# The seven-product pairs of an FFN: token sums traced ahead of the third chunk into buffers of their own, bank evacuations ranked above weight casts

## The chip, the cores and the metric

The kernel runs on one core of a Trainium2 chip. The metric is the device time of one execution in microseconds (us). Before the change the median of three runs is 990.08 us (989.32 to 993.01).

## The reference

Two layers of a streaming encoder on 256 tokens of width 1024, in float32. Each layer has three sub-layers: a feed-forward block (FFN), a mixer of attention and mLSTM, and a second FFN. What matters here is the FFN, of which four are computed:

```python
def _swiglu(h, w_in, w_out):
    gate, up = jnp.split(h @ w_in, 2, axis=-1)      # 1024 -> 2 x 2816
    return (jax.nn.silu(gate) * up) @ w_out         # 2816 -> 1024

x += 1/2 * post(SwiGLU_1(pre(x)))
x += post(W_out [DiffAttn | mLSTM](pre(x)))
x += 1/2 * post(SwiGLU_2(pre(x)))
```

`pre` and `post` are RMS norms. The weights are read from HBM once in each sub-layer.

## The kernel before

**Products.** Every product of float32 numbers is made of three TensorE matmuls on rounded halves, high and low: xh·wh, xh·wl, xl·wh (L471 to L473). So each weight has to be split on the chip. A piece of weights is 1 MB and is fetched on SyncE's queue (`fetch`, three buffers `wr`); each of its two halves is cast by ScalarE into `wh` (L296) and then subtracted by VectorE into `wl` (L297) (`halved`). This split runs through the whole kernel: 372 such pairs of instructions.

**The FFN.** The 2816 hidden columns are eleven chunks of 256. Chunks 0 and 1 come first, then a list of steps runs:

```python
STEPS = "I2 O0 I3 O1 P4 O2 I6 O3 I7 O4 O5 P8 O6 O7 I10"
```

`I` is the input product of a chunk (banks `ptr` for I2, `pin` for I3, in turn), `O` adds a chunk's part to the output banks `bk`, and `P` is a pair of chunks made with seven products instead of eight, in the manner of Strassen. After an `I` step `ffn_hidden` makes h: ScalarE's silu into `sil`, then VectorE multiplies by the other half of the bank (L598), and with that the bank is free. `ffn_planes` turns h around for the output product: ScalarE copies planes (L605), SyncE starts a transposing DMA (L607), ScalarE copies the result into `hT` (L609), and it is split into `hh` and `hl` (L624, L625). The last chunk, I10, is made the other way round (`in_turned`, `ffn_turned`), and behind it stands the ending, in which PE's order is written by hand.

**A pair.** P4 and P8 need sums of weights (`pair_blocks`, L314, VectorE; then 14 halves are split) and sums of tokens (`pair_tokens`): s1 to s4, ten VectorE instructions (L344 to L352) and for each sum a cast on ScalarE (L624, out `both`) and a subtraction on VectorE (L625, out `both`). The token sums are made once in an FFN, at P4, and P8 uses them again. Each of the seven products is twelve matmuls (L705). P1 and P2 use the tokens as they are and share one `pin` bank, so P1's result has to be copied out (`p1`, L717) before P2 adds to the bank; P5 (s1) and P6 (s2) go into a `ptr` and the other `pin` bank, P7 (s3) into the second `ptr` bank, to which P4 later adds, and P3 (s4) adds to P5's. `u`, `v`, `sil` and `h` take the results out.

**What sets the order.** The program is traced in the order of the code, and a scheduler then places each engine's instructions by its own timeline and a priority, which follows the order of tracing; `high_priority()` ranks a block ahead of all else. Each engine then runs its list strictly in order. Tiles come from rings: `u`, `v` and `sum` share a ring of five, "ev", with `h`, `planes`, `turned`, `hT` and others; what has no ring of its own, `sil` and `p1` among them, is in "k2" with four.

Of the kernel before, what the change touches and what calls it, by code (L numbers as in the profile page):

```python
# [20 lines left out]
AF = mybir.ActivationFunctionType  # L21
ALU = mybir.AluOpType
# [3 lines left out]
P = 128  # L26
# [11 lines left out]
END = (8, 9, 10)  # L38
# [97 lines left out]
class _Trunk:  # L136
# [12 lines left out]
        return f"{s}_{self.n}"  # L149


    TAGS = {"kwn": ("kwn", 1), "aT0": ("aT0", 1), "aT1": ("aT1", 1)}
    for _n in ("nat", "ra", "rb", "rv", "tmp", "y", "so", "xg", "h", "planes", "turned", "hT", "u", "v", "sum"):
        TAGS[_n] = ("ev", 5)

    def t2(self, nm, shape=(P, 512), dt=F32):
        tag, bufs = self.TAGS.get(nm, ("k2", 4))
        return self.k2.tile(list(shape), dt, tag=tag, bufs=bufs, name=self.name(nm))
# [502 lines left out]
    def ffn(self, pre, gi_post):  # L661
        xT, r = pre

        def in_piece(t, kh, pin, w):
            xh, xl = xT[t][kh]
            for k in range(4):
                self.mm3(pin, xh[:, k, :], xl[:, k, :], *self.cols(w, k),
                         start=kh == 0 and k == 0, stop=kh == 1 and k == 3)
# [23 lines left out]
        def ready(h):  # L692
            hT = self.ffn_planes(h.rearrange("p t j -> p (t j)"))
            return self.ffn_split([hT[:, t] for t in range(NT)])
# [7 lines left out]
        def product(b, x, w, new):  # L702
            for k in range(4):
                for n, (st, mv) in enumerate(((x[0], 0), (x[0], 1), (x[1], 0))):
                    self.nc.tensor.matmul(b, st[:, k, :], self.cols(w, k)[mv], start=new and k == n == 0,  # L705
                                          stop=k == 3 and n == 2, skip_group_check=True)

        def pair(c):


            tt, stt = self.nc.vector.tensor_tensor, self.nc.vector.scalar_tensor_tensor
            w = self.pair_blocks()
            b1, b2, b3, b4 = self.bank_pin(), self.bank_pin(), self.bank_tr(), self.bank_tr()
            s1, s2, s3, s4 = sums
            product(b1, xT[0][0], w["P1"], True)
            p1 = self.t2("p1")
            self.nc.scalar.activation(p1, b1, AF.Copy)  # L717
            product(b4, s1, w["P5"], True)
            product(b2, s2, w["P6"], True)
            u, v, h0, sil = self.t2("u"), self.t2("v"), self.t2("h"), self.t2("sil")  # L720
            tt(u, b2, p1, op=ALU.subtract)
            product(b3, s3, w["P7"], True)
            tt(v, u, b3, op=ALU.subtract)
            tt(v, v, b4, op=ALU.add)
            product(b1, xT[0][1], w["P2"], False)
            self.func(sil, b1, AF.Silu, scale=r[0])
            product(b4, s4, w["P3"], False)
            tt(h0, b4, u, op=ALU.add)
            stt(h0, h0, r[0], sil, op0=ALU.mult, op1=ALU.mult)
            hT = [self.ffn_planes(h0)]  # L730
            product(b3, xT[1][1], w["P4"], False)
            tt(u, b3, u, op=ALU.subtract)
            self.func(u, u, AF.Silu, scale=r[1])
            stt(v, v, r[1], u, op0=ALU.mult, op1=ALU.mult)
            hT.append(self.ffn_planes(v))
            for j in range(2):
                hs[c + j] = self.ffn_split([h[:, j] for h in hT])

        hs, po = {}, []
# [20 lines left out]
        else:  # L760
# [6 lines left out]
            h = self.t2("h", (P, NT, 256))  # L767
# [12 lines left out]
            h = self.t2("h", (P, NT, 256))  # L780
# [2 lines left out]
            in_piece(1, 1, pb1, w1[1])  # L783
            self.ffn_hidden(pb1, r[1], h[:, 1])
            hs[1] = ready(h)
        both, sums, swap = list(self.both), None, 0
        for step in STEPS[:-1]:
            c = int(step[1:])
            if step[0] == "P":
                sums = sums or self.pair_tokens(both)  # L790
                pair(c)
            elif step[0] == "I":
                if c == 3:
                    g = self.load_gpost(gi_post)
                    yield "middle"
                ws = [self.piece(), self.piece()]
                pins = [self.bank_pin() if swap else self.bank_tr() for _ in range(NT)]
                swap = 1 - swap
                for kh in range(2):
                    for t in range(NT):  # L800
                        in_piece(t, kh, pins[t], ws[kh])
                chunk(c, pins)
            else:
                if not po:
                    po = [[self.bank_bk() for _ in range(2)] for _ in range(NT)]
                wo = self.piece()
                for t in range(NT):
                    out_part(c, t, hs[c], wo)
        ws = [self.piece(), self.piece()]
        rows = self.token_scales(r)  # L810
        last = [self.piece() for _ in END[:-1]]
        banks = [[self.bank_pin() for _ in range(2)], [self.bank_tr() for _ in range(2)]]
        in_turned(banks, ws, both)

        yield "ending"
        hs[END[-1]] = self.ffn_turned(banks, rows)
        last.append(self.piece())
        for c, wo in zip(END, last):
            out_part(c, 0, hs[c], wo)
# [63 lines left out]
class _Mixer:  # L883
# [325 lines left out]
    def scores(self, t, h0):  # L1209

        tr, nc = self.tr, self.tr.nc
        nk, nh = P * (t + 1), 4 // (t + 1)
        if h0 == 0:
            self.aT[t] = tr.t2(f"aT{t}", (P, t + 1, 4, P))
            self.mx = tr.small("mx", (P, 2, 4))
            self.lsum[t] = tr.small("lsum", (P, 2, 4))
        hs = slice(h0, h0 + nh)
        pcs = [tr.bank_bk((P, nh, nk)) for _ in range(2)]
        for h in range(nh):
            for c in range(2):  # L1220
                rows = slice(c * 64, c * 64 + 64)
                self.mm(pcs[c][:, h, :], self.qkT[0][rows, h0 + h, t * P:(t + 1) * P],
                        self.qkT[1][rows, h0 + h, 0:nk], start=True, stop=True)
        for c in range(2):
            nc.vector.memset(pcs[c][0:64, :, nk - 64:nk], BIG)
            nc.vector.tensor_reduce(self.mx[:, c, hs], pcs[c], axis=AX.X, op=ALU.max, negate=True)
        if t:
            p = [tr.t2("p", (P, 2, nk)) for _ in range(nh)]
        else:
            ts = [tr.t2("p", (P, 2, 2, nk)) for _ in range(nh // 2)]  # L1230
            p = [ts[h // 2][:, h % 2] for h in range(nh)]
        self.p[t, h0] = p
        for h in range(nh):
            for c in range(2):
                tr.func(p[h][:, c, :], pcs[c][:, h, :], AF.Exp, bias=self.mx[:, c, h0 + h:h0 + h + 1],
                                accum_out=self.lsum[t][:, c, h0 + h:h0 + h + 1])

    def combine(self, t, h0):

        tr, nc, l = self.tr, self.tr.nc, self.l  # L1240
        nk, nh = P * (t + 1), 4 // (t + 1)
        hs = slice(h0, h0 + nh)
        lsum, aT = self.lsum[t], self.aT[t]
        c1 = tr.small("c1", (P, nh))
        nc.vector.reciprocal(c1, lsum[:, 1, hs])
        self.stt(c1, c1, tr.neglam[:, l:l + 1], lsum[:, 0, hs], op0=ALU.mult, op1=ALU.mult)
        ptr = tr.bank_tr((P, t + 1, nh, P))
        for h in range(nh):
            p = self.p[t, h0][h]
            self.stt(p[:, 0, :], p[:, 1, :], c1[:, h:h + 1], p[:, 0, :], op0=ALU.mult, op1=ALU.add)  # L1250
            for kt in range(t + 1):
                self.T(ptr[:, kt, h, :], p[:, 0, kt * P:(kt + 1) * P], tr.ident)
        self.act(aT[:, :, hs, :], ptr, AF.Copy)

    def attend(self, t):
        tr, l = self.tr, self.l
        po = tr.bank_bk((P, 4, P))
        for h in range(4):
            for kt in range(t + 1):
                self.mm(po[:, h, :], self.aT[t][:, kt, h, :], self.vd[:, kt, h * P:(h + 1) * P],  # L1260
                        start=kt == 0, stop=kt == t)
        ss = tr.small("ssa", (P, 4))
        for h in range(4):
            self.act(tr.junk_tile(P), po[:, h, :], AF.Square, scale=2.0 ** -3.5, accum_out=ss[:, h:h + 1])
        l2 = tr.small("l2", (P, 4))
        self.tt(l2, self.lsum[t][:, 0, :], self.lsum[t][:, 0, :], op=ALU.mult)
        self.stt(ss, l2, EPS, ss, op0=ALU.mult, op1=ALU.add)
        sc = tr.rsqrt(ss, 4)
        y = tr.t2("y", (P, 4, P))
        self.tt(y, po, sc.unsqueeze(2).broadcast_to([P, 4, P]), op=ALU.mult)  # L1270
        self.y[t] = y
# [113 lines left out]
```

## Time and profile before

| | |
|---|---|
| median of three runs | 990.08 us (989.32 to 993.01) |
| the profiled execution | 990.41 us, its span 988.6 us |
| TensorE (PE) busy | 950.4 us, 96% of the span |
| VectorE (DVE) busy | 788.2 us, 80% |
| ScalarE (ACT) busy | 669.5 us, 68% |
| mean granted PE clock | 0.983 of full |
| HBM read | 177.01 MB, 180 GB/s over the span |

Busy shares are means over the whole kernel. PE is the engine on which the end rests nearly everywhere, so what counts is the time in which PE waits or runs at a lower clock, and where that lies.

### The profile page before, as it was taken

The numbers are of one execution on the slowest core, as the hardware profiler recorded it, in microseconds if no ns is written. First come the engines' busy times: TensorE is split into PE (matmuls) and PEld (weight loads), VectorE is DVE, ScalarE is ACT, GpSimd is POOL, SyncE is SP. The second block draws the span as 40 slices with busy tenths as digits, with TensorE's granted clock in tenths as the row PEclk, the third lists the DMA queues.
The fourth block names the chain that finished last, engine by engine and source line by source line (L and its number), as shares of the span: only waits on it lengthen the run. The fifth ranks groups of instructions, "written<-read, shape, count | busy, mean of one in ns | idle before, by whom it ended". The sixth has DMA issues, their size and how long they took to land.

```text
span 988.6 us, 12155 instructions
## 1 busy us (share of the span) xinstructions
PE 950.4 (96%) x4427; PEld 778.7 (79%) x4427; DVE 788.2 (80%) x1097; ACT 669.5 (68%) x1033; POOL 29.3 (3%) x55
## 2 busy tenths in 40 slices
PE   9989999899999998999999799999999999899997
PEld 7867888787888876888788678888888888678886
DVE  6798797589766799698577977977898687997964
ACT  8875686478765775686567747765778468656862
POOL 2000000000010000000000000000000200000000
PEclk9998999999999999999999999999999999999999
DMA  8945668435352745757638446583364438556551
GB/s 324 340 130 198 211 213 291 116 127 193 129 213 85 280 141 194 237 171 272 196 118 308 149 167 202 185 304 101 128 234 140 159 135 298 178 208 196 170 178 43
DMA packets 69882, 189.34 MB, mean 192 GB/s; under 512 B 45274, under 2 KB 46426, under 8 KB 49086
## 3 DMA queue, kind: packets, MB, share of 16 engines
q1 hardware_dynamic: 69246, 187.95, 56.0%
q8 instruction: 35, 0.57, 0.2%
q10 hardware_dynamic: 576, 0.61, 0.2%
q14 instruction: 25, 0.20, 0.1%
HBM read 177.01 MB, written 1.05 MB: 180 GB/s over the span
## 4 chain that ended last, share of the span: by engine, by line
PE 73%; DVE 10%; ACT 8%; DMA 6%; issue 3%; SPq 0%; POOLq 0%; DVEq 0%; ACTq 0%
PE ptr L705 9%; PE bk L473 8%; PE bk L472 8%; PE bk L471 8%; PE pin L471 8%; PE pin L473 8%; PE pin L472 8%; PE pin L705 5%; DVE wl L297 5%; DMA turned<-planes 4%; ACT wh L296 3%; DMA wr<-in_w_dram 2%; PE ptr L471 2%; PE ptr L472 2%; PE ptr L473 2%
## 5 line engine op out<-in xcount | busy, mean ns | idle before, releaser
L297 DVE TENSOR_TENSOR wl<-wr,wh 128x1024 fp32r<-128x1024 f32 x324 | 386.6, 1219 | 69.4 <-ACT wh L296 68.6
L296 ACT ACTIVATE wh<-wr 128x1024 fp32r<-128x1024 f32 x324 | 331.2, 1053 | 96.0 <-DMA wr<-in_w_dram 33.6
L471 PE MATMUL pin<-wh,both 128*128 128x512 f32 x432 | 171.3, 398 | 0.0
L473 PE MATMUL pin<-wh,both 128*128 128x512 f32 x432 | 168.4, 390 | 0.0
L472 PE MATMUL pin<-wl,both 128*128 128x512 f32 x432 | 168.4, 390 | 0.0
L473 PE MATMUL bk<-wh,hl 128*128 128x512 f32 x352 | 138.6, 394 | 2.1 <-DVE hl L625 2.1
L471 PE MATMUL bk<-wh,hh 128*128 128x512 f32 x352 | 133.3, 395 | 5.4 <-ACT hh L624 3.1
L472 PE MATMUL bk<-wl,hh 128*128 128x512 f32 x352 | 138.1, 393 | 0.0
L705 PE MATMUL ptr<-wh,both 128*128 128x512 f32 x256 | 88.9, 411 | 11.4 <-ACT both L624 7.5
L473 PEld LDWEIGHTS pin<-wh,both 128*128 128x128 f32 x432 | 81.1, 188 | 17.4
L471 PEld LDWEIGHTS pin<-wh,both 128*128 128x128 f32 x432 | 81.3, 188 | 17.0 <-issue 0.7
L472 PEld LDWEIGHTS pin<-wl,both 128*128 128x128 f32 x432 | 81.2, 188 | 15.5
L609 ACT ACTIVATE hT<-turned 128x1024 uint16<-128x1024 uint16 x40 | 54.9, 1373 | 56.7 <-DMA turned<-planes 56.5
L471 PEld LDWEIGHTS bk<-wh,hh 128*128 128x128 f32 x352 | 66.7, 190 | 21.2 <-ACT hh L624 4.2
L473 PEld LDWEIGHTS bk<-wh,hl 128*128 128x128 f32 x352 | 66.9, 190 | 17.4 <-DVE hl L625 3.4
L472 PEld LDWEIGHTS bk<-wl,hh 128*128 128x128 f32 x352 | 66.8, 190 | 13.8
L705 PE MATMUL pin<-wh,both 128*128 128x512 f32 x192 | 66.7, 409 | 10.2 <-ACT p L717 9.1
L705 PEld LDWEIGHTS ptr<-wh,both 128*128 128x128 f32 x256 | 50.2, 197 | 25.5 <-ACT both L624 9.2
L297 DVE TENSOR_TENSOR wl<-wide,wh 128x1024 fp32r<-128x1024 f32 x48 | 57.7, 1217 | 2.5 <-ACT wh L296 2.1
L296 ACT ACTIVATE wh<-wide 128x1024 fp32r<-128x1024 f32 x48 | 49.4, 1049 | 13.3 <-DVE wide L314 8.0
L625 DVE TENSOR_TENSOR hl<-hT,hh 128x256 fp32r<-128x256 f32 x80 | 30.9, 418 | 32.8 <-ACT hh L624 32.8
L705 PEld LDWEIGHTS pin<-wh,both 128*128 128x128 f32 x192 | 38.1, 199 | 21.0 <-ACT p L717 10.8
(242 smaller groups left out, 1395.6 us busy)
## 6 DMA issues: line engine op xcount, KB each, us to landing
wr<-in_w_dram SPq DMA_DIRECT2D x162, 1024.0 KB, 5.0
gpost<-in_gpost_dram SPq DMA_DIRECT2D x6, 512.0 KB, 6.4
wr<-in_w_dram SPq DMA_DIRECT2D x2, 512.0 KB, 5.6
wr<-in_w_dram SPq DMA_DIRECT2D x3, 256.0 KB, 4.3
x<-in_x_dram SPq DMA_DIRECT2D x3, 256.0 KB, 4.7
turned<-planes SPq DMA_TRANSPOSE x40, 4.4
out_dram<-x SPq DMA_DIRECT2D x2, 256.0 KB, 2.1
x<-in_x_dram SPq DMA_DIRECT2D x2, 128.0 KB, 2.8
```

The source lines that it names most:

```text
L296: ia = nc.scalar.activation(hi, raw, AF.Copy)
L297: iv = nc.vector.tensor_tensor(lo, raw, hi.bitcast(F32), op=ALU.subtract)
L471: mm(ps, xh, wh, start=start, stop=False)
L472: mm(ps, xh, wl, start=False, stop=False)
L473: mm(ps, xl, wh, start=False, stop=stop)
L609: nc.scalar.activation(hT.rearrange("p a b n -> p (a b n)").bitcast(U16).rearrange("p (n u) -> p u n", u=2), turned.rearrange("p (u b) n - ...
L625: self.nc.vector.tensor_tensor(hl, h, hh.bitcast(F32), op=ALU.subtract)
L705: self.nc.tensor.matmul(b, st[:, k, :], self.cols(w, k)[mv], start=new and k == n == 0, stop=k == 3 and n == 2, skip_group_check=True)
```

## The change

It has four parts. The rings: "ev" goes from five to eight buffers and loses `u`, `v` and `sum`, which go into the ring "k2" of four beside `sil` and `p1`; the mixer's `aT` tiles lose their own buffers, go into "ev", and are split into one tile per 128 keys (so that ScalarE has four copies more in the whole kernel). The token sums: `pair_tokens` is called ahead of the loop over STEPS, so ahead of I2, and no longer inside it at P4. The evacuations of a pair (`p1`, `u`, `v`, `sil`, `h0` and the last ones) are put under `high_priority()`, with their tiles allocated ahead of the products. `ffn_turned`, too, is put under `high_priority()`.

```diff
-    TAGS = {"kwn": ("kwn", 1), "aT0": ("aT0", 1), "aT1": ("aT1", 1)}
-    for _n in ("nat", "ra", "rb", "rv", "tmp", "y", "so", "xg", "h", "planes", "turned", "hT", "u", "v", "sum"):
-        TAGS[_n] = ("ev", 5)
+    TAGS = {"kwn": ("kwn", 1)}
+    for _n in ("nat", "ra", "rb", "rv", "tmp", "y", "so", "xg", "h", "planes", "turned", "hT", "aT"):
+        TAGS[_n] = ("ev", 8)
@@ pair
+            ahead = self.tc.high_priority
+            p1, sil, u, v, h0 = self.t2("p1"), self.t2("sil"), self.t2("u"), self.t2("v"), self.t2("h")
             product(b1, xT[0][0], w["P1"], True)
-            p1 = self.t2("p1")
-            self.nc.scalar.activation(p1, b1, AF.Copy)
+            with ahead():
+                self.nc.scalar.activation(p1, b1, AF.Copy)
             product(b4, s1, w["P5"], True)
             product(b2, s2, w["P6"], True)
-            u, v, h0, sil = self.t2("u"), self.t2("v"), self.t2("h"), self.t2("sil")
-            tt(u, b2, p1, op=ALU.subtract)
+            with ahead():
+                tt(u, b2, p1, op=ALU.subtract)
...
@@ ffn
-        both, sums, swap = list(self.both), None, 0
+        both, swap = list(self.both), 0
+        sums = self.pair_tokens(both)
         for step in STEPS[:-1]:
             c = int(step[1:])
             if step[0] == "P":
-                sums = sums or self.pair_tokens(both)
                 pair(c)
...
-        hs[END[-1]] = self.ffn_turned(banks, rows)
+        with self.tc.high_priority():
+            hs[END[-1]] = self.ffn_turned(banks, rows)
@@ combine
-        self.act(aT[:, :, hs, :], ptr, AF.Copy)
+        for kt in range(t + 1):
+            self.act(aT[kt][:, hs, :], ptr[:, kt], AF.Copy)
```

What the scheduler makes of it is seen in the lists of the engines. In the rows below, the number behind a name tells apart the tiles of one name.

VectorE in the first FFN, behind the weights of I2 (`wl_498` before, `wl_524` after). `h_376` is chunk 1's h, `hl_299` and `hl_301` are chunk 0's. Before:

```order
L297 TENSOR_TENSOR wl_498<-wr_492,wh_499 128x1024
L205 TENSOR_TENSOR c_wgc<-c_528,c_wgc 128x16x8
L225 TENSOR_REDUCE c_hot<-c_95 100x4
L598 SCALAR_TENSOR_TENSOR h_376<-pin_326,rs_31_274,sil_377 128x256
L598 SCALAR_TENSOR_TENSOR h_376<-pin_327,rs_36_283,sil_380 128x256
L239 CAST c_hotp<-c_hot 36x256
L625 TENSOR_TENSOR hl_299<-hT_296,hh_298 128x256
```

And after:

```order
L297 TENSOR_TENSOR wl_524<-wr_518,wh_525 128x1024
L344 TENSOR_TENSOR sum_399<-both_129,both_187 128x512
L345 TENSOR_TENSOR sum_400<-both_129,both_187 128x512
L205 TENSOR_TENSOR c_wgc<-c_554,c_wgc 128x16x8
L225 TENSOR_REDUCE c_hot<-c_95 100x4
L598 SCALAR_TENSOR_TENSOR h_376<-pin_326,rs_31_274,sil_377 128x256
L598 SCALAR_TENSOR_TENSOR h_376<-pin_327,rs_36_283,sil_380 128x256
L346 TENSOR_TENSOR sum_399<-sum_399,sum_400 128x512
L239 CAST c_hotp<-c_hot 36x256
L625 TENSOR_TENSOR hl_299<-hT_296,hh_298 128x256
```

The fourteen VectorE instructions of the sums now stand between here and the first weights of P4, among the weights of I2 and I3; before, they stood among the weights of P4.

VectorE in the second FFN (the one behind the first mixer), at P4. `h_3336` before and `h_3365` after are the h of chunk 3, which frees the two `pin` banks of I3; `wl` of `wide`, `wr_3419` and `wr_3462` (before; 3422, 3443, 3465 after) are weights of P4. Before:

```order
L297 TENSOR_TENSOR wl_3444<-wide_3429,wh_3445 128x1024
L598 SCALAR_TENSOR_TENSOR h_3336<-pin_3286,rs_589_2923,sil_3337 128x256
L297 TENSOR_TENSOR wl_3448<-wide_3429,wh_3449 128x1024
L314 TENSOR_TENSOR wide_3429<-wide_3429,wr_3462 128x1024
L297 TENSOR_TENSOR wl_3454<-wr_3419,wh_3455 128x1024
L598 SCALAR_TENSOR_TENSOR h_3336<-pin_3287,rs_614_3010,sil_3340 128x256
L314 TENSOR_TENSOR wide_3429<-wide_3429,wr_3462 128x1024
```

And after:

```order
L297 TENSOR_TENSOR wl_3471<-wr_3465,wh_3472 128x1024
L297 TENSOR_TENSOR wl_3467<-wr_3465,wh_3468 128x1024
L297 TENSOR_TENSOR wl_3475<-wr_3443,wh_3476 128x1024
L314 TENSOR_TENSOR wide_3432<-wide_3432,wr_3465 128x1024
L297 TENSOR_TENSOR wl_3479<-wr_3443,wh_3480 128x1024
L297 TENSOR_TENSOR wl_3485<-wide_3432,wh_3486 128x1024
L598 SCALAR_TENSOR_TENSOR h_3365<-pin_3315,rs_590_2926,sil_3366 128x256
L598 SCALAR_TENSOR_TENSOR h_3365<-pin_3316,rs_615_3013,sil_3369 128x256
```

The first half of the same h moved behind ten more splits and sums of P4's weights, its second half behind seven. It is so in the third and the fourth FFN too; in the first it isn't.

TensorE at the start of the same P4: the last rows of the output step and the first product. `pin_3490` is the bank of P1, `ptr_3496` that of P5, `both_3138` holds s1 and s2, `both_2863` (before) the tokens. Before:

```order
L473 MATMUL bk_3229<-wh_3364,hl_3130 128x512
L705 MATMUL pin_3490<-wh_3422,both_2863 128x512
L705 MATMUL pin_3490<-wl_3421,both_2863 128x512
L705 MATMUL pin_3490<-wh_3422,both_2863 128x512 x2
L705 MATMUL pin_3490<-wl_3421,both_2863 128x512
```

And after:

```order
L473 MATMUL bk_3258<-wh_3393,hl_3133 128x512
L705 MATMUL ptr_3496<-wh_3436,both_3138 128x512
L705 MATMUL ptr_3496<-wl_3435,both_3138 128x512
L705 MATMUL ptr_3496<-wh_3436,both_3138 128x512 x2
L705 MATMUL ptr_3496<-wl_3435,both_3138 128x512
```

In the second, third and fourth FFN the pair now begins with P5 and P7 in the `ptr` banks (24 matmuls), and P1 and P6 in the `pin` banks follow; then comes the output step O2, and then P2. Before, P1 and P2 came first, 24 matmuls in one bank. In the first FFN the order after is P1, P5, P6 and P7 mixed, P2; before, P1, P2, P5, P6, P7.

More of the change, by code (lines that the diff above doesn't have):

```diff
@@ L714, in pair @@
             s1, s2, s3, s4 = sums
+            ahead = self.tc.high_priority
+            p1, sil, u, v, h0 = self.t2("p1"), self.t2("sil"), self.t2("u"), self.t2("v"), self.t2("h")
             product(b1, xT[0][0], w["P1"], True)
-            p1 = self.t2("p1")
-            self.nc.scalar.activation(p1, b1, AF.Copy)
+            with ahead():
+                self.nc.scalar.activation(p1, b1, AF.Copy)
             product(b4, s1, w["P5"], True)
             product(b2, s2, w["P6"], True)
-            u, v, h0, sil = self.t2("u"), self.t2("v"), self.t2("h"), self.t2("sil")
-            tt(u, b2, p1, op=ALU.subtract)
+            with ahead():
+                tt(u, b2, p1, op=ALU.subtract)
             product(b3, s3, w["P7"], True)
-            tt(v, u, b3, op=ALU.subtract)
-            tt(v, v, b4, op=ALU.add)
+            with ahead():
+                tt(v, u, b3, op=ALU.subtract)
+                tt(v, v, b4, op=ALU.add)
             product(b1, xT[0][1], w["P2"], False)
-            self.func(sil, b1, AF.Silu, scale=r[0])
+            with ahead():
+                self.func(sil, b1, AF.Silu, scale=r[0])
             product(b4, s4, w["P3"], False)
-            tt(h0, b4, u, op=ALU.add)
-            stt(h0, h0, r[0], sil, op0=ALU.mult, op1=ALU.mult)
+            with ahead():
+                tt(h0, b4, u, op=ALU.add)
+                stt(h0, h0, r[0], sil, op0=ALU.mult, op1=ALU.mult)
             hT = [self.ffn_planes(h0)]
             product(b3, xT[1][1], w["P4"], False)
-            tt(u, b3, u, op=ALU.subtract)
-            self.func(u, u, AF.Silu, scale=r[1])
-            stt(v, v, r[1], u, op0=ALU.mult, op1=ALU.mult)
+            with ahead():
+                tt(u, b3, u, op=ALU.subtract)
+                self.func(u, u, AF.Silu, scale=r[1])
+                stt(v, v, r[1], u, op0=ALU.mult, op1=ALU.mult)
             hT.append(self.ffn_planes(v))
@@ L1213, in scores @@
         if h0 == 0:
-            self.aT[t] = tr.t2(f"aT{t}", (P, t + 1, 4, P))
+            self.aT[t] = [tr.t2("aT", (P, 4, P)) for _ in range(t + 1)]
             self.mx = tr.small("mx", (P, 2, 4))
@@ L1259, in attend @@
             for kt in range(t + 1):
-                self.mm(po[:, h, :], self.aT[t][:, kt, h, :], self.vd[:, kt, h * P:(h + 1) * P],
+                self.mm(po[:, h, :], self.aT[t][kt][:, h, :], self.vd[:, kt, h * P:(h + 1) * P],
                         start=kt == 0, stop=kt == t)
```

## Prediction

> **What bounds the kernel now.** I read the shares of the engines first, then what PE waits for, then the stretches of the four P4 pairs, then VectorE's list ahead of them.
>
> ```profile
> span 988.6 us, 12155 instructions
> PE 950.4 (96%) x4427; PEld 778.7 (79%) x4427; DVE 788.2 (80%) x1097; ACT 669.5 (68%) x1033; POOL 29.3 (3%) x55
> ```
>
> PE is the bound, with 38 us of the span not busy. The list of what its matmuls waited for shows where:
>
> ```profile
> PE pin L705 <- ACT p L717: 9.1, 4, 3.1
> PE ptr L705 <- ACT both L624: 7.5, 4, 2.5
> PE ptr L705 <- DVE both L625: 3.9, 3, 1.6
> PE bk L471 <- ACT hh L624: 3.1, 2, 1.6
> PE bk L473 <- DVE hl L625: 2.1, 3, 0.9
> ```
>
> The first three rows (20.5 us) are the pair's: P2 waits for the copy of P1 four times, once in each FFN, and P5 to P7 wait for the casts and remainders of the token sums. The last two are mostly the endings. Around the largest of these waits PE's records in the first FFN (start, length, form, idle time before) read:
>
> ```profile
> 67.92 0.63 PE L705 MATMUL pin<-wh,both 128*128 128x512 f32 x1 [3.06 <-ACT p L717]
> 68.35 0.63 PE L705 MATMUL pin<-wl,both 128*128 128x512 f32 x1
> 74.77 0.66 PE L705 MATMUL ptr<-wh,both 128*128 128x512 f32 x1 [2.24 <-ACT both L624]
> 77.43 1.22 PE L705 MATMUL ptr<-wh,both 128*128 128x512 f32 x2 [1.58 <-DVE both L625]
> ```
>
> Behind such a wait the matmuls follow each other at 0.43 us (67.92 to 68.35). The chain of work that ended last gives the same for a group (start, length, what; the first group is right behind the third wait, the second is undisturbed):
>
> ```profile
> 77.43 4.57 PE ptr L705 x10
> ...
> 86.10 2.27 PE ptr L705 x10
> ```
>
> That is 0.457 us a matmul against 0.227, half the clock, until the stretch ends. Ten cost 2.3 us more here, the twelve from 67.92 on about 1.7. So a wait costs itself and about 1.7 us behind it. By stretches (us, PE busy, granted clock; four P4 pairs, then two endings):
>
> ```profile
> 60.00:90.00 30.00, 23.12 (x82) 0.83 0.43 149
> 365.00:395.00 30.00, 25.14 (x100) 0.94 0.53 175
> 555.00:585.00 30.00, 23.72 (x88) 0.89 0.44 150
> 850.00:880.00 30.00, 24.86 (x100) 0.94 0.49 154
> 178.00:193.00 15.00, 12.51 (x47) 0.89 0.34 131
> 478.00:493.00 15.00, 12.76 (x51) 0.89 0.44 149
> ```
>
> In the first, 6.9 us are idle, and the clock falls short of full by 0.17 x 30 = 5.1 us, of which the two groups above are 4.0 (the rest lies over idle time): 10.9 lost. With the same share (0.78) of the other shortfalls of 1.8, 3.3 and 1.8 us the pairs of the other FFNs lose 4.9 + 1.4 = 6.3, 6.3 + 2.6 = 8.9 and 5.1 + 1.4 = 6.5; together 32.6 us. The two endings lose 2.5 + 1.3 and 2.2 + 1.3. This is all that the change can touch; the P8 pairs show no wait.
>
> **Why the pair waits.** VectorE is full there (start to end, its busy time; first the stretch ahead of P4 in the first FFN, then P4, then the stretches ahead of P4 in the other three):
>
> ```profile
> 20.00:62.00 42.00, 35.38 (x44) 1.00 0.85 275
> 62.00:85.00 23.00, 22.96 (x29) 0.78 0.42 148
> 337.40:367.00 29.60, 26.52 (x32) 1.00 0.50 169
> 526.00:555.60 29.60, 27.04 (x32) 1.00 0.54 174
> 824.50:854.30 29.80, 27.15 (x32) 1.00 0.56 175
> ```
>
> The durations of what it does, start to start, are in the chain:
>
> ```profile
> 63.48 1.14 DVE wide L314
> 64.62 3.41 DVE wl L297 x3
> 68.02 0.60 DVE sum L344
> ```
>
> The fourteen instructions of the token sums are 14 x 0.60 = 8.4 us of VectorE, in the middle of P4's weights.
>
> **The change, part by part.** Moving the sums takes 8.4 us out of P4 and puts them into the stretch ahead. That removes the waits for `both`, if VectorE has room there. It has 6.6 us idle in the first FFN (42.00 - 35.38) and only 3.1, 2.6 and 2.7 in the others; the part for which there is no room makes P4's weights late instead. The four casts of the sums on ScalarE (68% busy) move with them, hidden beside the weight casts. No DMA is moved except that in the first FFN two pieces stand ahead of loads of constants that wait for nothing; I cost that at nothing.
>
> First FFN. Of the idle time I count 5.4 us as usable, the waits for hh, lamv and two casts that lie behind the place of the new rows:
>
> ```profile
> DVE hl L625 <- ACT hh L624: 3.0, 1, 3.0
> DVE lamp L216 <- DMA lamv<-in_lam_dram: 1.4, 1, 1.4
> DVE wl L297 <- ACT wh L296: 0.5, 1, 0.5
> DVE c_wgc L205 <- ACT c_wgc L204: 0.5, 1, 0.5
> ```
>
> So VectorE comes to P4's weights 8.4 - 5.4 = 3.0 us late, at 63.0 for the weight that it split at 60.0, and then runs without the sums. PE's new order puts P5 between P1 and P2, so the 3.06 us for P1's copy go. What is late next is v, which reads P7's bank before the product P4 may add to it: from 63.0, in the row of after, eight splits, two sums of weights, two hl, u and three further splits, 13 x 1.14 + 0.7 + 0.6, so v runs from 79.1 to 79.8; PE, from 62.0 with 60 matmuls of the five products and four of O2, is there at 62.0 + 64 x 0.227 = 76.5. A wait of 3.5 with 1.7 behind it: 5.2 in place of 10.9, **-5.7** (ends: -10.9 if v isn't late, 0 if two such waits are left).
>
> Second FFN. The starts in question (PE: first of P4 in the second, third and fourth FFN; VectorE: an h of chunk 1 in each, from which I walk, and the idle times that can still be filled):
>
> ```profile
> L705 PE MATMUL pin<-wh,both x24: 387/394/796, 367.0 to 384.9; 128*128 128x512 f32 x24
> L705 PE MATMUL pin<-wh,both x24: 388/389/628, 555.6 to 575.1; 128*128 128x512 f32 x24
> L705 PE MATMUL pin<-wh,both x24: 388/389/547, 854.3 to 872.6; 128*128 128x512 f32 x24
> 337.00 0.48 DVE L598 SCALAR_TENSOR_TENSOR h<-pin,rs,sil 128x256 f32<-128x256 f32 x1
> 530.62 0.48 DVE L598 SCALAR_TENSOR_TENSOR h<-pin,rs,sil 128x256 f32<-128x256 f32 x1
> 828.69 0.48 DVE L598 SCALAR_TENSOR_TENSOR h<-pin,rs,sil 128x256 f32<-128x256 f32 x1
> ```
>
> Here chunk 3's h is the last thing of I3 and now stands behind ten more of P4's rows, while PE does P5 and P7 (24 matmuls, 5.45 us) and then needs the bank that this h frees. VectorE's list of after from the row of 337.0 to the end of h: 25 splits and sums of weights x 1.135, 14 x 0.605, 4 x 0.34, 6 x 0.4 = 40.6, so 377.6 if no idle time is left, 379.3 with what I cannot place; PE is ready at 367.0 + 5.45 = 372.4. A wait of 5.2 to 6.9, I take 6.0, and 1.7 behind it: 7.7 against 6.3, **+1.4**. Third FFN, by the same walk from 530.62: 33.8, with 0.2 of lag brought along, 564.6; PE ready at 561.0; wait 4.0 with the semaphores' way, and 1.7: 5.7 against 8.9, **-3.2**. Fourth, from 828.69: 32.6, so 861.3 to 861.6; PE ready at 859.8; 2.2 and 1.7: 3.9 against 6.5, **-2.6**. Ends for the three together: +8, if the copy of P1 behind the late bank also holds P2, and -14.
>
> The priority of the evacuations acts where the scheduler had put them behind weight casts; P2 now has O2 or two products ahead of it (at least 24 matmuls, 5.4 us), so the copy's 0.57 us is covered. The cover would be gone only if the copy waits for ScalarE's `hT` of chunk 3, which the late h delays by its transposition; 24 matmuls of P6 and O2 lie over that.
>
> Endings. `ffn_turned` ahead of casts moves the hh for which the output product waits one cast earlier (1.05 us in its row):
>
> ```profile
> L296 ACT ACTIVATE wh<-wr 128x1024 fp32r<-128x1024 f32 x324 | 331.2, 1053 | 96.0 <-DMA wr<-in_w_dram 33.6 <-PE ptr L705 20.1 <-PE bk L473 14.6
> ```
>
> That is about 1.0 in each of the two endings that wait, **-2.0** (0 to -6). The rings and the split `aT`: four ScalarE copies more, in mixers where PE hardly waits: 0 (ends -1 and +2).
>
> The sum: -5.7 + 1.4 - 3.2 - 2.6 - 2.0 = -12.1. Against the profiled execution's 990.41 this is 978.3, and, the median of the runs being 0.3 lower, **978**.
>
> [...]
>
> **The rivals.** (B) The waits nearly all go: VectorE's lag is absorbed, because the weights of P4 are split before PE needs them. Then 32.6 + 4 are gained: 954, or two thirds of it, 966. Against it: VectorE had 3 us idle where 8.4 go. (C) The gain is given back: what the sums cost at P4 is now the lag of weights and of h, in three of four FFNs. With the first FFN at -3, the others at 0 and the endings at nothing: 985 to 995. For it: the three rows of 26.5 to 27.2 busy out of 29.6. (D) Slower: chunk 3's h holds the `pin` banks in three FFNs so long that P1, P6 and then P2 each wait. It decides from the point where each FFN loses 12 us and not 6: one wait of 7, its 1.7, and a second of 3 to 4 for the copy behind `hT`; 3 x 5 = +15, less 8 of the first FFN and the endings, 997. Against it: the walk puts h 1.8 to 5.2 us behind PE, not 7.
>
> **How the numbers follow.** A forecast sum within 966 to 985: 0.64. B below 966: 0.08. C, 985 to 995: 0.17. D above 995: 0.11. A measurement of this kernel tells about 0.5%, 5 us, from no change; so faster (below 985) 0.72, same 0.17, slower 0.11. The range leaves out the larger part of B and the far half of D with the edge of C: 964 to 993.
>
> **What would show it.** Right: at P4 no row of PE waiting for `both` from L624 or L625; in the first FFN one wait of 3 to 4 us at a `ptr` bank for v; in the second one of some 6 us at `pin` for chunk 3's h (L598), in the third 4, in the fourth 2; the endings' waits near 1.5 instead of 2.5. Wrong: if P5 itself waits for its weights, if the copy of P1 still shows with 2 us or more, or if waits appear at P8, in the steps I6 and I7, or in the mixers, where I cost the rings at nothing.

## The result and the profile after

The changed kernel takes 983.55 us in the median (983.13 to 984.71, four runs) against 990.31 us before on the same chip: ratio 0.9926, 95% interval 0.9903 to 0.9949. That is 6.8 us less, where 12.1 had been forecast. The page of the profile after, in its first lines:

```profile
span 981.5 us, 12114 instructions
PE 946.0 (96%) x4427; PEld 776.0 (79%) x4427; DVE 787.5 (80%) x1097; ACT 666.7 (68%) x1037; POOL 28.5 (3%) x55
```

The work is the same; what PE waited for is not (us in total, times, longest):

```profile
PE bk L471 <- ACT hh L624: 9.0, 4, 3.7
PE pin L705 <- DVE h L598: 8.8, 3, 5.4
PE ptr L705 <- DVE v L726: 2.0, 1, 2.0
PE bk L473 <- DVE hl L625: 1.8, 3, 0.9
PE ptr L705 <- DVE wl L297: 1.4, 2, 1.1
...
PE pin L705 <- ACT p L719: 0.8, 1, 0.8
```

The waits for the token sums (the 7.5 and 3.9 us of L624 and L625 for `both`) are gone, and of the 9.1 us for P1's copy 0.8 are left. In their place stand 8.8 us for chunk 3's h, three times, and the wait for hh at the output product has gone from 3.1 to 9.0 us. Stretch by stretch (length, PE busy, granted clock: the four P4 pairs, then the first three endings):

```profile
60.00:90.00 30.00, 26.94 (x108) 0.94 0.55 190
368.00:398.00 30.00, 23.73 (x93) 0.89 0.66 206
547.00:577.00 30.00, 25.87 (x112) 1.00 0.49 142
844.00:874.00 30.00, 28.52 (x125) 1.00 0.60 175
173.00:188.00 15.00, 12.51 (x42) 0.77 0.37 140
477.00:492.00 15.00, 9.44 (x26) 0.77 0.52 175
665.00:680.00 15.00, 12.82 (x59) 1.00 0.51 175
```

Three of the P4 pairs are better, the second FFN's is worse, and so are the endings: in the second, PE was busy 9.4 us of 15. The third ending before read:

```profile
665.00:680.00 15.00, 14.47 (x73) 1.00 0.64 228
```

For the comparison of all kernels I use one measure: the time by which PE's matmuls of 512 columns, start to start, exceed 0.25 us, which is a tenth more than the 0.227 us that one takes undisturbed (those of 256 columns, most of which follow each other at 0.12 us, count likewise from a tenth above 0.115). It holds waits and low clock together, and "loses" below means this measure. One profiled execution each, us:

| kernel | P4 pairs, FFN 1 to 4 | their sum | the rest of each FFN with its ending | its sum | all |
|---|---|---|---|---|---|
| before | 11.2, 7.3, 10.7, 7.2 | 36.4 | 4.5, 4.3, 1.0, 0.1 | 9.9 | 54.2 |
| after | 5.4, 8.8, 4.8, 1.9 | 20.8 | 5.7, 9.4, 2.8, 0.1 | 18.0 | 47.7 |

So P4 gained 15.6 us and the endings gave back 8.1; 1.0 went elsewhere.

### The profile page after: what moved, and what is told of

Its sections match the earlier page's. It is cut to its first block, busy times and chain, and to the rows that moved or that the text cites. A ratio compares the mean times of both kernels' runs of the same rounds, so it can differ in the third digit from the quotient of the medians.

```text
span 981.5 us, 12114 instructions
## 1 busy us (share of the span) xinstructions
PE 946.0 (96%) x4427; PEld 776.0 (79%) x4427; DVE 787.5 (80%) x1097; ACT 666.7 (68%) x1037; POOL 28.5 (3%) x55
## 4 chain that ended last, share of the span: by engine, by line
PE 53%; DVE 24%; DMA 10%; ACT 8%; issue 4%; SPq 0%; POOLq 0%; DVEq 0%; ACTq 0%
DVE wl L297 12%; PE bk L473 6%; PE pin L471 6%; PE bk L472 6%; PE pin L473 6%; PE pin L472 6%; PE bk L471 6%; DMA wr<-in_w_dram 5%; DMA turned<-planes 5%; PE ptr L705 4%; PE pin L705 3%; DVE wide L314 3%; ACT wh L296 3%; PE ptr L471 2%; PE ptr L473 2%
## 5 line engine op out<-in xcount | busy, mean ns | idle before, releaser
L705 PE MATMUL ptr<-wh,both 128*128 128x512 f32 x256 | 84.1, 394 | 2.0 <-DVE v L726 2.0
L705 PE MATMUL ptr<-wl,both 128*128 128x512 f32 x128 | 50.8, 397 | 1.4 <-DVE wl L297 1.4
```

## The experiments

**The evacuations' priority, taken away (no_evac).**

```diff
-            ahead = self.tc.high_priority
+            ahead = contextlib.nullcontext
```

> The changed kernel with the evacuations of the pairs at their plain priority again (rings, early token sums and the priority of ffn_turned stay). Theory 1: the priority of the evacuations is what spoils the endings. It puts u (and its silu on ScalarE) ahead of the last multiplication of h0 and of the copy of its planes, so the first transposition of the P8 pair starts late and hh comes late for the output product. Then the losses of the three endings (5.6, 9.4 and 2.7 us in the changed kernel) go back to about 4.4, 4.3 and 0.9, and the time is 975 to 977; the P4 pairs keep their waits for chunk 3's h (8.8 us). Rival: PE comes to the endings earlier, while weights and transpositions are paced by the DMA, so that the wait appears whatever the order: then the endings lose as much as now and the time stays at 982 to 985.

Measured: 973.39 us, ratio 0.9825 (0.9794 to 0.9855), 10 us faster than the change. P4 loses 5.5, 6.9, 5.1 and 1.9, the endings 4.4, 1.7, 4.0 and 0.1: 10.2 in place of 18.0. The wait for h is still there, that for hh has more than halved:

```profile
PE pin L705 <- DVE h L598: 8.5, 3, 5.2
PE bk L471 <- ACT hh L624: 3.9, 3, 1.8
```

Theory 1 stands for the sum, and PE's early arrival alone is not the reason: PE comes earlier still here. It missed the third ending, which loses 4.0 us in place of 2.8. What the priority does is seen at the P8 pair of the second FFN. VectorE's and ScalarE's records of this pair (other rows between them left out), before:

```profile
461.96 0.68 DVE L728 TENSOR_TENSOR h<-ptr,u 128x512 f32<-128x512 f32 x1
463.69 0.74 DVE L729 SCALAR_TENSOR_TENSOR h<-h,rs,sil 128x512 f32<-128x512 f32 x1
464.35 0.68 DVE L732 TENSOR_TENSOR u<-ptr,u 128x512 f32<-128x512 f32 x1
464.47 1.06 ACT L605 ACTIVATE planes<-h 128x1024 uint16<-128x1024 uint16 x1 [0.43 <-DVE h L729]
```

and after:

```profile
463.40 0.69 DVE L733 TENSOR_TENSOR h<-ptr,u 128x512 f32<-128x512 f32 x1
466.26 0.69 DVE L738 TENSOR_TENSOR u<-ptr,u 128x512 f32<-128x512 f32 x1
466.86 0.75 DVE L734 SCALAR_TENSOR_TENSOR h<-h,rs,sil 128x512 f32<-128x512 f32 x1
466.99 0.73 ACT L268 ACTIVATE u<-u,rs 128x512 f32<-128x512 f32 x1 [3.43 <-DVE u L738]
467.62 1.04 ACT L296 ACTIVATE wh<-wr 128x1024 fp32r<-128x1024 f32 x1
468.56 1.04 ACT L605 ACTIVATE planes<-h 128x1024 uint16<-128x1024 uint16 x1
```

u has passed h's last multiplication, and on ScalarE its silu stands ahead of the planes of h. From the first h to the planes it is 5.2 us in place of 2.5 (in no_evac 453.89 to 456.81, 2.9). The planes start the transposition (`turned`), and the second transposition waits behind the first on ScalarE: v is ready at 468.5, but its planes start at 477.02, behind the copy `hT` of the first at 475.80. The chain of work at this ending, after:

```profile
469.63 6.15 DMA turned<-planes
...
475.80 1.35 ACT hT L609
...
482.04 1.24 ACT hT L609
```

The first h itself also comes later against PE's products: between v (L724 before, L727 after) and it stand five splits in place of four. How much of the ending is that, and how much the swap, these runs don't separate.

**Only its last block taken away (lastplain).** A build in which h0's block alone loses the priority has the same lists on every engine as the change, so that block does nothing. The same holds for the blocks of the first u, of v and of `sil`. The priority of P1's copy moves it ahead of one weight cast on ScalarE, in five places. What is left is the last block:

```diff
-            with ahead():
-                tt(u, b3, u, op=ALU.subtract)
-                self.func(u, u, AF.Silu, scale=r[1])
-                stt(v, v, r[1], u, op0=ALU.mult, op1=ALU.mult)
+            tt(u, b3, u, op=ALU.subtract)
+            self.func(u, u, AF.Silu, scale=r[1])
+            stt(v, v, r[1], u, op0=ALU.mult, op1=ALU.mult)
```

> The changed kernel with the plain priority for the last block of the pair alone (u from the third bank, its silu, the last multiplication of v); p1, the first u and v, sil and h0 keep theirs. Theory 1, narrowed: this block alone lets u and its silu pass h0, so the endings come back as with no priority at all, 971 to 977. Rival: the price is that of the whole set of priorities, and half of it or more stays: 979 or above.

Measured: 972.93 us, ratio 0.9821 (0.9790 to 0.9851): as without any. The endings lose 8.8 us (3.0, 4.4, 1.3 and 0.1). Three lines held the whole price. Against no_evac only those five places on ScalarE's list differ, yet there the second and third endings lost 1.7 and 4.0: single endings move by some 2.7 us between two such kernels, and their sum by 1.4. So the sums count here, not each ending.

**The priority on the kernel before (evac_only).** The function `pair` of after, the rest of before.

> The kernel before with the priority of the pairs' evacuations alone. Theory 1: nothing is gained at P4 (the waits for the token sums stay, 20 us in all), and the endings lose 6 to 8 us more: 995 to 998. Rival (the endings are late because PE is early): no change at the endings, 988 to 991, or less if the copy of P1 comes sooner.

Measured: 991.28 us, ratio 1.0003 (0.9981 to 1.0026). Theory 1 missed here, and the time is the rival's to 0.3 us. In the profiled execution the endings lose 12.8 in place of 9.9 and P4 37.4 in place of 36.4, but at 994.50 us it is the second slowest of twelve, and the median shows no price. Yet u passes h's last multiplication here too: at the P8 pair of the second FFN the first h starts at 460.37 and its planes at 466.85, 6.5 us later. So the swap alone is not the price; what it costs depends on the order around it, and in what way stays open.

**The early sums alone (sums_only).**

```diff
-        both, sums, swap = list(self.both), None, 0
+        both, swap = list(self.both), 0
+        sums = self.pair_tokens(both)
...
-                sums = sums or self.pair_tokens(both)
```

> The kernel before with the token sums traced ahead of the loop, in the old rings (sums, u and v in the ring of five with h, planes and hT), no priorities. Theory 2: the sums' buffers hold up chunk 2's and chunk 3's h whatever the ring, as long as they share it with something of these chunks; here they share it with h itself, and h of chunk 3 stands last of P4's list on VectorE in the three later FFNs. So waits for chunk 3's h at P4 of 8 to 14 us, endings as before: 978 to 986. Rival: the early sums bring the whole gain at P4 by themselves and the rings cost it: 970 or below.

Measured: 989.94 us, ratio 0.9987 (0.9970 to 1.0003): nothing. Both expectations missed. P4 loses 6.3, 10.3, 11.4 and 10.4 (the endings some 7 in place of 9.9), and what PE waits for isn't h but the sums themselves:

```profile
PE ptr L705 <- DVE both L625: 15.5, 3, 6.1
PE ptr L705 <- ACT both L624: 8.6, 3, 3.5
```

Though traced ahead of the loop, they stand among P4's weights again. VectorE in the second FFN, where PE began P4 at 359.2:

```profile
357.09 0.68 DVE L344 TENSOR_TENSOR sum<-both 128x512 f32<-128x512 f32 x1
...
369.96 1.28 DVE L625 TENSOR_TENSOR both<-sum,both 128x512 fp32r<-128x512 f32 x2
371.17 0.86 DVE L598 SCALAR_TENSOR_TENSOR h<-pin,rs,sil 128x256 f32<-128x256 f32 x2
```

The first sum starts at 343.12, ahead of P4, where before it stood behind P4's start; but the last remainder ends at 371.2, 12 us after PE began P4. The late h that had been expected is there too, right behind it, where PE has already waited. In this kernel the sums share the ring of five with h, planes and hT. The place in the trace brought them forward, but not ahead of P4; that the ring held them is argued here and tested below.

**The rings alone (rings).** The new rings with `aT` split, on the kernel before.

> The kernel before with the change's rings alone (ev of eight without u, v and sum, these in the ring of four with sil and p1; aT split and in ev). Theory 2: the token sums now wait for buffers that chunk 2's and chunk 3's silu tiles hold, and stand as late on VectorE as before; so P4 keeps 20 to 30 us of losses and the time is 982 to 992. Rival: the rings are what shortens P4, 975 or below.

Measured: 995.45 us, ratio 1.0042 (1.0018 to 1.0067), a little slower, and above the 982 to 992 expected. P4 loses 35.8 us, hardly less than before (36.4), and the waits for `both` stay. The endings lose 15.7 in place of 9.9; that was not expected, and no run here shows why.

**A ring of its own for silu (sil6).** The late h after the change: its silu tiles share the ring "k2" of four with the six tiles of the sums. With the evacuations' priority taken away as in no_evac, and:

```diff
-    TAGS = {"kwn": ("kwn", 1)}
+    TAGS = {"kwn": ("kwn", 1), "sil": ("sl", 2)}
-        TAGS[_n] = ("ev", 8)
+        TAGS[_n] = ("ev", 6)
```

> The changed kernel without the evacuations' priority, and with a ring of two for the silu tiles, so that they no longer share a ring with the token sums (for room, the ring ev has six buffers instead of eight). Theory 2: the late h of chunk 3 comes from silu tiles that wait for buffers held by the sums; with their own ring h stands ahead of most of P4's weights, the 8.8 us of PE's waits for h (L598) go to under 2, and with the endings back the time is 966 to 970. Rival: VectorE has no room (2.6 to 3.1 us idle for 8.4), so P4's weights come late instead and PE waits as long for wl: 974 to 978.

Measured: 957.61 us, ratio 0.9662 (0.9633 to 0.9691), 16 us below no_evac and more than I had expected. No wait for h is left; P4 loses 5.2 us in the first FFN and 0.0 in the other three. The largest waits now:

```profile
PE bk L471 <- ACT hh L624: 3.3, 2, 1.8
PE bk L472 <- DVE wl L297: 2.1, 1, 2.1
PE bk L473 <- DVE hl L625: 1.7, 2, 0.9
```

That "ev" has six buffers here is not the cause: with six and the old "k2", the build has the same lists as no_evac.

**The same with the sums traced at P4 (sil6_late).**

> The fastest kernel so far (silu tiles in a ring of their own, no priorities for the evacuations) with pair_tokens traced at P4 again, as before the change. Theory 3: what holds the sums is not their place in the trace but a ring shared with tiles of chunks 2 and 3; once they share none, the scheduler places them early by itself. Then VectorE's list hardly differs and the time is 956 to 962. Rival: the place in the trace is what counts: the waits for the sums' casts come back and the time is 975 to 985.

Measured: 957.68 us, ratio 0.9669 (0.9642 to 0.9695). The same time, with the second part of the change undone. Once the sums share no ring with the tiles of chunks 2 and 3, the scheduler places them early by itself: in the second FFN VectorE is through with them at 344.1, and PE begins P4 at 365.5.

**The same with the priority (sil6_evac).**

> The fastest kernel so far with the priority of the pairs' evacuations put back. Theory 1: u stands ahead of h0's last multiplication again, the endings lose 3 to 8 us more, and nothing is gained at P4: 961 to 966. Rival: the price of the priority came from the late h of chunk 3 and is gone with it: 956 to 959.

Measured: 959.70 us, ratio 0.9688 (0.9663 to 0.9714). The endings lose 12.8 in place of 10.4, and 2 us in the times lie within the intervals: less than the 3 to 8 expected, and not settled by the time alone.

**A ring for the sums in place of silu (sum5).** Against the change:

```diff
-    TAGS = {"kwn": ("kwn", 1)}
+    TAGS = {"kwn": ("kwn", 1), "sum": ("sm", 3)}
-        TAGS[_n] = ("ev", 8)
+        TAGS[_n] = ("ev", 5)
-            ahead = self.tc.high_priority
+            ahead = contextlib.nullcontext
```

> The changed kernel without the evacuations' priority, with a ring of three for the token sums (ev has five buffers) in place of a ring for silu. Theory 2: what counts is that sums and silu tiles share no ring, whichever gets one of its own; the later P4 pairs lose 0 to 2 us and the time is 955 to 962. Rival: with three buffers the sums are held by each other and come later: waits for both at P4, 965 to 972.

Measured: 956.09 us, ratio 0.9652 (0.9624 to 0.9680), the fastest, though not told apart from sil6. The later P4 pairs lose 0.0. VectorE has the last sum ready long before PE's P4, which begins at 359.0, and chunk 3's h in time:

```profile
342.11 0.68 DVE L625 TENSOR_TENSOR both<-sum,both 128x512 fp32r<-128x512 f32 x1
...
357.42 0.48 DVE L598 SCALAR_TENSOR_TENSOR h<-pin,rs,sil 128x256 f32<-128x256 f32 x1
...
361.21 0.48 DVE L598 SCALAR_TENSOR_TENSOR h<-pin,rs,sil 128x256 f32<-128x256 f32 x1
```

## Why the prediction came out as it did

The direction and the range held; the 978 was 5.5 us too low, and that is the sum of two errors of opposite sign: P4 gained 5.5 us more than forecast, and the endings came out 10.1 worse. That the forecast came so near is partly luck. By its terms (P4 by the measure above, us):

| term | forecast | measured |
|---|---|---|
| P4, first FFN | -5.7 | 11.2 to 5.4: -5.8 |
| P4, second | +1.4 | 7.3 to 8.8: +1.5 |
| P4, third | -3.2 | 10.7 to 4.8: -5.9 |
| P4, fourth | -2.6 | 7.2 to 1.9: -5.3 |
| endings | -2.0 | 9.9 to 18.0: +8.1 |
| elsewhere | 0 | +1.0 |

**P4.** Each wait was where the walk along VectorE's list had put it. PE's records, the waits of the first, second, third and fourth FFN:

```profile
81.28 0.50 PE L705 MATMUL ptr<-wh,both 128*128 128x512 f32 x1 [2.04 <-DVE v L726]
374.22 0.77 PE L705 MATMUL pin<-wh,both 128*128 128x512 f32 x1 [5.43 <-DVE h L598]
567.87 0.47 PE L705 MATMUL pin<-wh,both 128*128 128x512 f32 x1 [2.23 <-DVE h L598]
860.23 0.47 PE L705 MATMUL pin<-wh,both 128*128 128x512 f32 x1 [1.10 <-DVE h L598]
```

Forecast were 3.5, 6.0, 4.0 and 2.2, so all four were shorter. The -5.8 of the first FFN is nearer to the forecast than its working: the wait was 1.5 us shorter, and three small ones that the walk didn't have (0.30, 0.35 and 0.37) made up for part of it. In the fourth FFN 1.9 us were lost in place of 3.9, above all because the 1.7 us that I put behind each wait did not come. In the third they did not come either, but two waits of about 1 us (at 562.85 and 575.31) took their place: 4.8 in place of 5.7. The larger part of the difference there is the state before, which I had put at 8.9 us where the measure above has 10.7. The forecast wait of 4.0 in the third has 0.4 in it for the semaphores' way, an estimate that no run shows: there PE's first matmul stands 0.15 us behind the end of h's first half (567.73 to 567.87).

**The endings: the step that failed.** I had written that `ffn_turned` ahead of casts moves the hh that is waited for one cast earlier. Built without that priority, the kernel has the same lists on all engines: this part of the change does nothing, and the term of -2.0 had no cause. And I had costed the evacuations' priority at P1's copy alone; the block that does act is the last one of the pair. That it costs 10 us of time, no_evac and lastplain show. That it does so by holding up the transposition on which the ending waits is read from the rows of one ending, and evac_only, with the same swap and no price that the times show, says that this is not all of it.

**The rivals.** B, that the waits nearly all go, was given 0.08, since "VectorE had 3 us idle where 8.4 go". That looked at the wrong place. Ahead of it, in the 30 us from 305, VectorE before was busy 23.11 us, so 6.9 us more were free. In sum5 that room is used: 26.51 us of the 30 from 300 are busy. Before:

```profile
305.00:335.00 30.00, 23.11 (x30) 1.00 0.54 196
```

With silu's ring apart and the rest of the change kept but for two buffers of "ev" (sil6_evac), 959.70 us was measured, within B's 954 to 966. So the late h, which I took as the price of a full VectorE, was the price of the change's own ring. C was right that gains are given back, not where. D did not come: one wait of 5.43, and no second behind it. The sentence against it put h 1.8 to 5.2 us behind PE, while the walk itself went up to 6.9, so D was nearer than it said.

## What to carry to other kernels

A tile ring is part of the order: with silu tiles and token sums in one ring PE waited 8.5 us for chunk 3's h (no_evac), with two rings not at all (sil6). So before moving work ahead in the code look at what shares its ring; here a ring of its own for the silu tiles was worth 16 us, and with it the place in the code nothing. A priority acts between neighbours: here it put one evacuation ahead of another that feeds a transposition, and cost 10 us in one kernel and nothing that the times show in two others. So ask of each ranked instruction whom it passes, and measure it in the kernel in which it is to stand. And build each part of a change alone first: parts that leave every engine's list the same need no price.

## What the runs showed of the hardware

Half the clock does not follow each wait. It stood behind one of 3.06 us before, and after the change behind one of 5.43, where the matmuls follow each other at 0.42 us (374.79 to 375.21):

```profile
374.79 0.63 PE L705 MATMUL pin<-wl,both 128*128 128x512 f32 x1
375.21 1.05 PE L705 MATMUL pin<-wh,both 128*128 128x512 f32 x2
```

Behind the 2.23 us of the third FFN the matmuls went on at 0.23 us:

```profile
568.18 0.39 PE L705 MATMUL pin<-wl,both 128*128 128x512 f32 x1
568.41 0.61 PE L705 MATMUL pin<-wh,both 128*128 128x512 f32 x2
```

But behind the 2.04 us of the first FFN, which has three small waits ahead of it (0.30, 0.35 and 0.37 us from 72.9 on), the matmuls from 82.4 to 85.3 were slow again, 0.43 us apart (82.35 to 82.78). So of these two waits the shorter one was followed by half the clock. In the traces of before and after the granted clock changes 15 and 9 times, from 68.14 to 986.32 us and from 82.28 to 979.98, and all these changes lie whole multiples of 3.41 us apart (the longest stretches between them, 293.55 and 488.11 us, are 86 and 143 of them). On this grid, the stretches around three of these waits read (start and end, length, PE busy, granted clock, and two columns for the DMA that are not used here; first the wait of 3.06 us before, then the waits of 2.04 and 2.23 us after):

```profile
64.73:68.13 3.40, 0.34 (x2) 1.00 0.79 289
68.14:71.55 3.41, 3.41 (x9) 0.50 0.05 19
...
78.86:82.27 3.41, 1.37 (x6) 1.00 0.43 180
82.28:85.69 3.41, 3.41 (x9) 0.50 0.65 207
...
563.56:566.96 3.40, 2.08 (x10) 1.00 0.87 304
566.97:570.38 3.41, 2.51 (x11) 1.00 0.86 308
570.39:573.79 3.40, 3.40 (x16) 1.00 1.22 125
```

The 2.04 us lie within one step of the grid, and PE was idle for 60% of it; the 2.23 us are split over two steps, 39% and 26%. The three small waits lie in earlier steps. Counted in the traces of before and after by PE's busy time, all 12 steps at full clock in which PE was idle for 1.93 us or more were followed by half the clock, and none of those with 1.63 us or less; of two with 1.81 us one was, the other not. In these two traces the border so lies at about half of a step. A step at half the clock in which PE has work throughout (68.14 to 71.55 above) costs half of its 3.41 us, and this is the 1.7 us of the prediction: the price was right, but in these traces it went with the idle time in one step, not with each wait.
